# Where the pools of an encoder block's tiles begin in SBUF

## The chip, the core and the metric

The kernel runs on one core of one Trainium2 chip. The metric is the device time of one execution in microseconds (us). A core has five engines that this text names as the profile does: PE (TensorE, the matmuls; PEld is its weight load), DVE (VectorE), ACT (ScalarE), POOL (GpSimd) and SP (SyncE, which here issues DMAs). SBUF is the on-chip memory of 128 partitions; an address in this text is a byte offset within a partition, the same in all 128.

## What is computed

One layer of a bidirectional encoder on 512 positions of width 2048, all in float32, batch 1:

```
h = rmsnorm(x);  z = h @ w_in                       # q latent | kv latent | rope key | conv b, c, h
q, k, v from the latents (8 heads, 128 + 64 rotary dimensions, values 128)
attn = softmax(q k^T / sqrt(192)) v
y = b * conv3(c * h)
x = x + concat(rmsnorm(attn), rmsnorm(y)) @ w_o
u = conv3(rmsnorm(x) @ w_ffn_up) + bias;  g, val = split(u)
x = x + (silu(g) * val) @ w_ffn_down                # d_ff = 5632
out = rmsnorm(x)
```

## The kernel before

The weights lie in DRAM as 375 units of 128 x 1024 float32 (512 KB). A unit is loaded by SP into a tile `raw` (line 261), rounded by ACT to a tile `hi` of the type float32r (line 234), and the remainder `raw - hi` is written by DVE to a tile `lo` (line 231). Activations are split in the same way into pairs of tiles of 128 x 512. A product of two float32 matrices is then three float32r matmuls per block of 128: hi with hi, hi with lo, lo with hi (`mm3`, lines 246 to 250, with the matmul at line 244, and `product`, lines 872 to 881, with the matmul at line 880).

On PE each matmul is two instructions: LDWEIGHTS reads 128 columns (512 bytes of a partition) of the stationary operand, and MATMUL streams the moving operand past it. The moving operand is a whole tile of 512 columns (2048 bytes) in the first part of the program, a half tile of 256 columns (1024 bytes) in the rest. In the profile both operands stand in a matmul's name, `ps<-t,hi`: moving `t`, weights `hi`. `ps<-t` alone means that both operands are `t` tiles.

The program runs through these stages, in this order:

- latent projections, short convolution and attention, output projection, and the first six blocks of the up-projection (line 244, 512 columns wide, but for the values of the attention, lines 547 to 567: there the roles are turned, `hi` and `lo` are the moving operands, 256 columns wide, and the latent's `t` tiles are the weights);
- the other 38 blocks of the up-projection (`up_seven`, line 880): 2 x 2 blocks by seven products in place of eight, moving operands of 256 columns;
- five chunks of the down-projection (`down_seven`, line 880), again by seven products; here each product writes two halves of a PSUM bank, 12 matmuls to each half;
- the last chunk of the down-projection and the final norm (`last_half`, line 244): 256 columns wide, weights and moving operands both in `t` tiles.

The order of the instructions on each engine is fixed by the scheduler when the program is built. What the change touches is where tiles lie. Tile pools take their space in SBUF one behind the other, in the order in which they are opened (lines 174 to 178): `cpool` (constants, vectors of gains), `tp` (80 tiles `t` of 2048 bytes, some of which are named `l`), `sp` (2 small tiles `st`), `wraw` (8 tiles `raw` of 4096 bytes), `wsp` (3 tiles `hi` and 3 tiles `lo` of 4096 bytes). So all `t` tiles have one and the same remainder when their address is divided by 512, and so have all slices of `raw`, `hi` and `lo`, as these are cut at multiples of 512 bytes.

Of the kernel before, what the change touches and what calls it, by code (L numbers as in the profile page):

```python
# [41 lines left out]
F32 = mybir.dt.float32  # L42
# [4 lines left out]
P = 128  # L47
# [15 lines left out]
SCALE = float(1.0 / np.sqrt(np.float32(NOPE + ROPE)))  # L63
UW = 1024
NT = 80
NPLAIN = 6
ORDER = [0, 1, 2, 3, 4]
EARLY = ()
# [103 lines left out]
def encoder_block(ctx: ExitStack, tc: tile.TileContext, gx, wall, vecs, rot, out):  # L172
    nc = tc.nc
    cpool = ctx.enter_context(tc.tile_pool(name="cpool", bufs=1))
    tp = ctx.enter_context(tc.tile_pool(name="tp", bufs=NT))
    sp = ctx.enter_context(tc.tile_pool(name="sp", bufs=2))
    wraw = ctx.enter_context(tc.tile_pool(name="wraw", bufs=8))
    wsp = ctx.enter_context(tc.tile_pool(name="wsp", bufs=3))
    dram = ctx.enter_context(tc.tile_pool(name="dram", bufs=1, space=bass.MemoryType.DRAM))
# [24 lines left out]
    ga = first[:, :KD]  # L204
    vec = cpool.tile([P, NVEC], F32, name="vec")
    nvec = cpool.tile([P, 3 * NF], F32, name="nvec")
    cs = []


# [605 lines left out]
    def up_plain(f, by_half):  # L815

        us, its = [None, None], []
        for s in range(2):
            def conv(ps, s=s):
                t = ztile()  # L820
                us[s] = ztile()
                if s == 0:
                    tt(t, ps, rx.r, ALU.mult)
                else:
                    nc.vector.scalar_tensor_tensor(out=t, in0=ps, scalar=-1.0, in1=rx.r, op0=ALU.mult, op1=ALU.mult)
                conv_up(us[s], t, s, f)

            lag = 5 if (f, s) == (0, 0) else 1
            its.append(proj16([("up", s, f, j) for j in range(2)], h2, [(lag, conv)] + [(lag + 1, lambda ps: gated(us, f))] * s, True))
        return its  # L830
# [121 lines left out]
    def up_seven(f):  # L952
        tg, tv, us = [], [], [None, None]

        def c11(ps):
            tg.append(ztile())
            nc.scalar.copy(out=half(tg[0], 0), in_=ps)

        def c22(ps, other):
            tv.append(ztile())  # L960
            tt(half(tv[0], 1), ps, other, ALU.add)

        def c21(ps, other):
            tt(half(tv[0], 0), ps, other, ALU.add)
            us[1] = ztile()
            conv_up(us[1], tv[0], 1, f)

        def c12(ps):
            nc.scalar.copy(out=half(tg[0], 1), in_=ps)
            us[0] = ztile()  # L970
            conv_up(us[0], tg[0], 0, f)

        units = {f"a{s + 1}{j + 1}": ("up", s, f, j) for s in range(2) for j in range(2)}
        its = seven(f, units, {"c11": c11, "c22": c22, "c21": c21, "c12": c12}, operands)
        its[-1].posts.append((2, lambda: gated(us, f)))
        return its
# [3 lines left out]
    plain = []  # L980
    for f in range(0, NPLAIN - 2):
        plain += [it for its in up_plain(f, False) for it in its]
    four = [it for f in range(NPLAIN - 2, NPLAIN) for it in up_plain(f, True)]
    plain += [its[j] for j in range(2) for its in four]
# [5 lines left out]
    items.extend(plain)  # L990
    for f in range(NPLAIN, NF):
        items.extend(up_seven(f))
# [146 lines left out]
```

## Time and profile before

| | |
|---|---|
| median of 3 runs | 2035.53 us (2034.5 to 2035.62) |
| profiled execution | 2035.79 us, its span 2034.0 us |
| PE busy | 1997.3 us (98%), 13826 matmuls |
| weight loads busy | 1848.2 us (91%) |
| DVE busy | 1542.0 us (76%) |
| ACT busy | 977.4 us (48%) |
| granted PE clock, mean | 0.992 |

The span runs from the first to the last instruction. A share of busy time says how long an engine had something in work; since matmuls are pipelined, the busy time of PE says less than the distance from the start of one matmul to the start of the next, which is had by dividing a stretch by the count of its matmuls. In the rows below "x" stands before a count, times without a unit are us, and PEclk is the granted clock as a share of 2.4 GHz.

### The profile page before, as it was taken

What the parts mean: (1) busy time and instruction counts of PE and PEld (TensorE: products, weight loads), DVE (VectorE), ACT (ScalarE), POOL (GpSimd) and SP (SyncE); (2) the same over time, 40 slices, a digit from 0 to 9 for tenths busy, and PEclk for the clock granted to TensorE, in tenths of its full rate; (3) what the DMA queues carried; (4) which work ended last, traced back from release to release, by engine and by line L of the source; (5) the groups of instructions that cost most, each with busy time, mean ns of one, the idle gap of its engine ahead of it and who ended that gap; (6) DMA issues with size and microseconds to landing.
All of it is one profiled execution on the core that took longest, in us unless ns stands there. A gap on an engine that the chain in (4) does not pass through costs nothing.

```text
span 2034.0 us, 33864 instructions
## 1 busy us (share of the span) xinstructions
PE 1997.3 (98%) x13826; PEld 1848.2 (91%) x13826; DVE 1542.0 (76%) x1893; ACT 977.4 (48%) x1358; POOL 209.6 (10%) x204
## 2 busy tenths in 40 slices
PE   8999999999999999999999999999997999999997
PEld 7888888888888888999999999999997999999997
DVE  7375877664556587788888888888887998987776
ACT  6253534433224344555555555555565554444454
POOL 5001232310001000000000000000010001000000
PEclk9999999999999999999999999999998999999998
DMA  7322222222444344445545545545557776677642
GB/s 259 100 86 78 78 78 73 73 91 95 133 138 140 130 156 138 136 134 152 171 136 151 170 137 150 172 138 148 170 143 219 225 197 172 186 187 199 179 116 83
DMA packets 94155, 290.78 MB, mean 143 GB/s; under 512 B 10672, under 2 KB 18992, under 8 KB 94000
## 3 DMA queue, kind: packets, MB, share of 16 engines
q1 hardware_dynamic: 77648, 230.95, 33.9%
q0 software_dynamic: 16352, 57.68, 13.7%
q8 instruction: 108, 1.77, 0.4%
q14 instruction: 47, 0.39, 0.1%
HBM read 267.62 MB, written 20.97 MB: 142 GB/s over the span
## 4 chain that ended last, share of the span: by engine, by line
PE 90%; DVE 4%; DMA 2%; issue 1%; ACT 0%; SPq 0%; DVEq 0%; ACTq 0%
PE ps L880 50%; PE ps L244 41%; DVE t L231 2%; DMA t<-act 2%; DVE lo L231 2%; DVE raw L231 0%; ACT hi L234 0%; DVE t L846 0%; SPq L787 0%; DVE t L845 0%; SPq L261 0%; DVE t L489 0%; DVEq L1134 0%; ACT ps L931 0%; ACT t L349 0%
## 5 line engine op out<-in xcount | busy, mean ns | idle before, releaser
L880 PE MATMUL ps<-t,hi 128*128 128x256 f32 x6496 | 1118.5, 278 | 17.7 <-ACT hi L234 7.2
L880 PEld LDWEIGHTS ps<-t,hi 128*128 128x128 f32 x6496 | 978.1, 188 | 20.3 <-DVE t L231 8.0
L234 ACT CAST hi<-raw 128x1024 fp32r<-128x1024 f32 (+1 forms) x544 | 568.3, 1047 | 702.9 <-PE ps L244 242.3
L880 PE MATMUL ps<-t,lo 128*128 128x256 f32 x3248 | 884.4, 278 | 1.9 <-DVE lo L231 1.9
L231 DVE TENSOR_TENSOR lo<-raw,hi 128x1024 fp32r<-128x1024 f32 (+1 forms) x543 | 668.4, 1232 | 198.4 <-ACT hi L234 188.3
L244 PE MATMUL ps<-t,hi 128*128 128x512 f32 x2096 | 654.3, 394 | 4.4 <-ACT t L239 3.5
L880 PEld LDWEIGHTS ps<-t,lo 128*128 128x128 f32 x3248 | 602.8, 188 | 2.6 <-DVE lo L231 2.5
L244 PEld LDWEIGHTS ps<-t,hi 128*128 128x128 f32 x2096 | 394.3, 189 | 92.0 <-ACT t L239 4.2
L244 PE MATMUL ps<-t,lo 128*128 128x512 f32 x1056 | 411.4, 392 | 0.0
L231 DVE TENSOR_TENSOR t<-ps,t 128x512 f32<-128x512 f32 (+3 forms) x255 | 143.0, 575 | 152.6 <-PE ps L244 99.8
L231 DVE TENSOR_TENSOR t<-t 128x512 fp32r<-128x512 f32 (+4 forms) x356 | 223.1, 645 | 34.2 <-DMA t<-act 13.2
L244 PEld LDWEIGHTS ps<-t,lo 128*128 128x128 f32 x1056 | 198.9, 188 | 45.0 <-issue 0.5
L231 DVE TENSOR_TENSOR raw<-raw 128x1024 f32<-128x1024 f32 x154 | 187.8, 1219 | 0.5
L244 PE MATMUL ps<-t 128*128 128x256 f32 (+1 forms) x642 | 108.6, 326 | 0.0
L234 ACT CAST t<-t 128x512 fp32r<-128x512 f32 (+2 forms) x149 | 81.3, 577 | 48.8 <-DVE t L231 25.1
L244 PEld LDWEIGHTS ps<-t 128*128 128x128 f32 x642 | 95.1, 190 | 10.3
L231 DVE TENSOR_TENSOR t<-t,ps 128x512 f32<-128x512 f32 x128 | 86.7, 683 | 21.1 <-PE ps L880 19.7
L782 POOL DMA_DIRECT2D act<-t x48 | 27.4, 570 | 694.4 <-DVE t L231 658.9
L231 POOL TENSOR_TENSOR t<-t 128x512 f32<-128x512 f32 x39 | 64.1, 1645 | 72.3 <-DVE t L231 40.5
L904 POOL DMA_DIRECT2D raw<-wall x58 | 50.3, 868 | 163.6 <-ACT t L936 69.4
L910 POOL DMA_DIRECT2D raw<-wall x20 | 17.1, 854 | 316.8 <-DVE lo L231 215.5
L343 ACT ACTIVATE t<-l 128x512 f32<-128x512 f32 x44 | 27.5, 626 | 45.7 <-DVE l L231 45.5
(81 smaller groups left out, 825.3 us busy)
## 6 DMA issues: line engine op xcount, KB each, us to landing
raw<-wall SPq DMA_DIRECT2D x372, 512.0 KB, 4.3
raw<-wall POOLq DMA_DIRECT2D x78, 512.0 KB, 7.4
act<-t POOLq DMA_DIRECT2D x48, 256.0 KB, 2.5
t<-act SPq DMA_DIRECT2D x48, 256.0 KB, 5.1
t<-gx SPq DMA_DIRECT2D x16, 256.0 KB, 3.8
xr<-l POOLq DMA_DIRECT2D x16, 256.0 KB, 2.4
t<-xr SPq DMA_DIRECT2D x16, 256.0 KB, 4.0
t<-xr SPq DMA_DIRECT2D x32, 128.0 KB, 3.9
```

The costliest lines, as they stand in the source:

```text
L231: (eng or nc.vector).tensor_tensor(out=o, in0=a, in1=b, op=op)
L234: nc.scalar.copy(out=dst[0], in_=src)
L244: nc.tensor.matmul(ps, lhsT=w, rhs=x, start=start, stop=stop)
L343: nc.scalar.activation(sq, src, AF.Square)
L782: nc.gpsimd.dma_start(o, t.bitcast(F32))
L880: nc.tensor.matmul(half(ps, e), lhsT=w[a][:, c:c + P], rhs=ops[k][q][b], start=start and e == k == i == 0, stop=k == n - 1 and i == 2, ski ...
L904: nc.gpsimd.dma_start(raw["a21"], wall[UIDX[units["a22"]]], accum_op=ALU.add)
L910: nc.gpsimd.dma_start(raw["s"], wall[UIDX[units["a12"]]], accum_op=ALU.add)
```

## The change

Two things move. `sp` is opened ahead of `tp`, and two tiles that nothing reads or writes take up space: `rest` (912 bytes, the last of `cpool`) and `space` (64 bytes, in a pool `gap` of its own between `tp` and `wraw`).

```diff
+REST = 228
+GAP = 16
...
     cpool = ctx.enter_context(tc.tile_pool(name="cpool", bufs=1))
+    sp = ctx.enter_context(tc.tile_pool(name="sp", bufs=2))
     tp = ctx.enter_context(tc.tile_pool(name="tp", bufs=NT))
-    sp = ctx.enter_context(tc.tile_pool(name="sp", bufs=2))
+    gap = ctx.enter_context(tc.tile_pool(name="gap", bufs=1))
     wraw = ctx.enter_context(tc.tile_pool(name="wraw", bufs=8))
     wsp = ctx.enter_context(tc.tile_pool(name="wsp", bufs=3))
...
     nvec = cpool.tile([P, 3 * NF], F32, name="nvec")
+
+    cpool.tile([P, REST], F32, name="rest")
+    gap.tile([P, GAP], F32, name="space")
     cs = []
```

The addresses in the two built programs:

| tiles | before: first address, remainder by 512 | now: first address, remainder by 512 |
|---|---|---|
| `t`, `l` | 6560, 416 | 7680, 0 |
| `raw` | 170592, 96 | 171584, 64 |
| `hi` | 203360, 96 | 204352, 64 |
| `lo` | 215648, 96 | 216640, 64 |
| `st` | 170400, 416 | 7488, 320 |
| `ones`, `ident`, `first`, `vec`, `nvec` | unchanged | unchanged |

Weights in `hi` or `lo` thus begin 192 bytes behind a moving operand in `t` before (96 - 416 + 512), and 64 bytes behind it now, both by remainders. Two `t` tiles stay 0 apart, and so do two of `raw`, `hi` and `lo`. Divided by 64, all of these addresses have the remainder 32 before and 0 now. No instruction is added or taken away, and none moves: on all five engines the built programs hold the same instructions with the same waits in the same order.

## Rows read from the trace of the kernel before

**Rows 1.** The profile's page: busy time by engine, and the chain by engine.
```profile
PE 1997.3 (98%) x13826; PEld 1848.2 (91%) x13826; DVE 1542.0 (76%) x1893; ACT 977.4 (48%) x1358; POOL 209.6 (10%) x204
...
PE 90%; DVE 4%; DMA 2%; issue 1%; ACT 0%; SPq 0%; DVEq 0%; ACTq 0%
```
**Rows 2.** Chain of waits in order of time: start, length, what, count of instructions.
```profile
46.29 779.53 PE ps L244 x3515
825.81 699.17 PE ps L880 x6169
...
1527.77 5.42 DMA t<-act
...
1572.45 25.72 PE ps L880 x216
...
1685.42 42.44 PE ps L880 x358
...
1766.54 189.74 PE ps L880 x1608
```
**Rows 3.** Windows: PE, PEld, DVE, ACT, POOL busy (count), PEclk, DMA share, GB/s.
```profile
0.00:46.00 46.00, 40.65 (x163) 32.91 (x163) 32.25 (x24) 28.89 (x43) 26.52 (x22) 0.93 0.76 277
550.00:700.00 150.00, 150.00 (x657) 123.06 (x656) 91.91 (x118) 51.93 (x65) 8.98 (x16) 1.00 0.41 139
826.00:1525.00 699.00, 699.00 (x6170) 699.00 (x6169) 578.04 (x625) 403.50 (x552) 54.20 (x76) 1.00 0.53 152
1558.00:1560.00 2.00, 2.00 (x11) 2.00 (x11) 1.97 (x6) 0.62 (x1) 0.00 (x0) 0.50 0.81 274
1766.00:1956.00 190.00, 189.46 (x1607) 189.45 (x1608) 156.39 (x181) 87.00 (x101) 15.82 (x19) 1.00 0.72 194
```
**Rows 4.** Timeline of PE, both operands in t tiles: start, length, what, count.
```profile
197.47 7.41 PE L244 MATMUL ps<-t 128*128 128x512 f32 x32
...
1978.78 21.04 PE L244 MATMUL ps<-t 128*128 128x256 f32 x174
```
**Rows 5.** Timeline of PE, the attention's values (moving hi, weights t), two heads' pairs.
```profile
150.27 0.39 PE L244 MATMUL ps<-hi,t 128*128 128x256 f32 x2
...
151.29 0.39 PE L244 MATMUL ps<-hi,t 128*128 128x256 f32 x2
...
248.98 0.40 PE L244 MATMUL ps<-hi,t 128*128 128x256 f32 x2
...
250.04 0.40 PE L244 MATMUL ps<-hi,t 128*128 128x256 f32 x2
```
**Rows 6.** Timeline of PE in the stretch at half clock.
```profile
1557.46 0.63 PE L880 MATMUL ps<-t,hi 128*128 128x256 f32 x2
...
1559.38 0.63 PE L880 MATMUL ps<-t,hi 128*128 128x256 f32 x2
```
**Rows 7.** Timeline of PEld, weight loads of matmuls one column wide.
```profile
446.29 0.86 PEld L244 LDWEIGHTS ps<-ones,t 128*128 128x128 f32 x7
```
**Rows 8.** Groups by line and shape: busy, mean ns, then idle before and releasers.
```profile
L231 DVE TENSOR_TENSOR lo<-raw,hi 128x1024 fp32r<-128x1024 f32 x537 | 662.5, 1235 | 198.4 <-ACT hi L234 188.3 <-PE ps L244 9.5
L244 PE MATMUL ps<-t,hi 128*128 128x512 f32 x2096 | 654.3, 394 | 4.4 <-ACT t L239 3.5 <-ACT hi L234 0.8
L234 ACT CAST hi<-raw 128x1024 fp32r<-128x1024 f32 x537 | 564.0, 1052 | 691.1 <-PE ps L880 237.1 <-PE ps L244 231.5 <-issue 167.9
L244 PE MATMUL ps<-t,lo 128*128 128x512 f32 x1056 | 411.4, 392 | 0.0
L231 DVE TENSOR_TENSOR raw<-raw 128x1024 f32<-128x1024 f32 x154 | 187.8, 1219 | 0.5
L231 DVE TENSOR_TENSOR t<-t 128x512 f32<-128x512 f32 x111 | 76.5, 698 | 4.4 <-ACT t L343 3.7 <-ACT t L387 0.2
...
L244 PE MATMUL ps<-t 128*128 128x512 f32 x258 | 60.9, 389 | 0.0
...
L244 PE MATMUL ps<-t 128*128 128x256 f32 x384 | 47.8, 284 | 0.0
...
L244 PEld LDWEIGHTS ps<-ones,t 128*128 128x128 f32 x64 | 8.2, 191 | 1.8 <-ACT t L349 0.6 <-POOL t L231 0.5 <-DVE t L231 0.3
```

## The prediction

> **What bounds the kernel now.** I read the page's busy times first: PE is at work for 98% of the span, its weight loads for 91%, DVE for 76%, and the chain that ended last is PE for 90% [rows 1]. Then the chain in order of time: two pieces, 779.53 us of 512-column work and 699.17 us of 256-column work, are PE without a break, and a third of 189.74 us lies in the down-projection [rows 2]. Only between 1525 and 1766 do DVE and transfers stand in the chain between pieces of PE. So the time is the number of matmuls times their spacing, and the views that count are those that give a spacing.
>
> The windows show the clock at full level (1.00, 2.4 GHz) in these stretches [rows 3]. At one column a cycle 256 columns take 106.7 ns and 512 take 213.3 ns. Against that:
>
> - Moving `t`, weights `hi`/`lo` (192 apart), 256 columns: 699.17 us over 6169 matmuls are 113.3 ns in the up-projection; 189.74 over 1608 are 118.0 ns in the down-projection [rows 2].
> - The same pair with 512 columns: 150.00 us with 656 weight loads, 228.7 ns [rows 3].
> - Both in `t` (0 apart): 512 columns, (7.41 - 0.39) / 31 = 226.5 ns, where 0.39 is the length of one such matmul; 256 columns, (21.04 - 0.28) / 173 = 120.0 ns, 0.28 being the length of one [rows 4, 8].
> - Moving `hi`, weights `t` (so 416 - 96 = 320 apart), 256 columns: nine matmuls in 1.02 us, 113.3 ns, at one place, and nine in 1.06 us, 117.8 ns, at another [rows 5].
> - At half clock (0.50, so 1.2 GHz) nine matmuls take 1.92 us, 213.3 ns: exactly the 256 columns, nothing over [rows 3, 6].
>
> Two things follow. What lies above the columns is no fixed cost of an instruction, since it is gone at half clock; it looks like operands that don't come fast enough at full clock. And it depends on where the operands lie: the same 256 columns cost 113.3 or 120.0 ns. In cycles the excess of 113.3, 120.0 and 226.5 is 16, 32 and about 32, and 16 columns of float32 are 64 bytes. So I read it as lumps of 64 bytes, though 118.0 and 228.7 are no whole number of them and must be mixtures (averages of 5/3 and 7/3 lumps).
>
> [...]
>
> **The change part by part.**
>
> *Instructions.* None is added, removed or moved, so there is no wait to follow along a queue; the two new tiles are never written. Cost 0.
>
> *DVE, ACT, POOL.* `raw`, `hi` and `lo` keep their distance to each other (0), `t` tiles to `t` tiles too. DVE takes 1235 ns for 1024 elements from `raw` and `hi`, 1219 ns in place on `raw`, 698 ns for 512 elements of `t` [rows 8]: 521 to 537 ns for the second 512, less than the first 512 cost, so nothing grows with the length as an excess would. I take 0. Even a per cent of them lies beside PE outside the 241 us from 1525 to 1766: at most about 2 us either way.
>
> *Transfers.* In the chain they stand at a few restores of `t` tiles such as 5.42 us [rows 2], 2% of the span [rows 1], about 41 us. A few per cent of that, for rows that begin on a rounder address, would be 1 us. I take 0.
>
> *512-column matmuls.* There are 2096 + 1056 = 3152 with `hi` or `lo` [rows 8]; of the 163 matmuls in the first 46 us, which wait for loads, 16 are the warm-up, so 147 of them don't count [rows 3], and 3005 are left. Bounds: from 228.7 down to the bare 213.3 is 15.4 ns each, 46 us; upward, a lump of 6.7 ns more would be 20 us. Between lies 226.5, the row of the same shape at distance 0, and one lump below that, 219.8, if rows that begin on a multiple of 64 touch one lump fewer. I take the middle of these two, 223.2: 3005 x 5.5 = 17 us saved.
>
> *256-column matmuls in the up-projection.* 6169 at 113.3 ns. Bounds: bare 106.7 saves 41 us, 120.0 costs 41 us. A floor of its own is the weight load: seven loads of one-column matmuls, which stream nothing, follow each other at (0.86 - 0.19) / 6 = 111.7 ns, 0.19 being the mean length of one [rows 7, 8]. So nearly nothing can be had unless the loads too get faster. I take 113.3 as it is, 0 us.
>
> *256-column matmuls in the down-projection.* The pieces of 216, 358 and 1608 run at 119.1, 118.5 and 118.0 ns with their first, longer one [rows 2]: about 2180 matmuls, with smaller pieces between 1565 and 1685 some 2350. The values of the attention show that 113.3 and 118 are two levels of one arrangement, between which chance seems to choose [rows 5]. Bounds: 118.0 to 111.7, 15 us saved, to 120.0, 5 us lost. I take 113.3, the level of the up-projection: 2350 x 4.7 = 11 us saved. DVE is busy 156.39 of 190 us there [rows 3], so it does not take over as the bound.
>
> *Matmuls with both operands in `t`.* Their distance stays 0; only the address modulo 64 changes. There are 384 with 256 columns and 258 with 512 [rows 8]: a lump each would be 4 us. I take 0 and keep them as the test.
>
> Sum: 2035.8 - 17 - 11 = 2008 from the profiled execution's 2035.79, which is 0.3 above the median of the runs; I predict 2009.
>
> **The rivals.**
>
> *A. Some of the excess goes* (as above): 512-column spacing between 219.8 and 226.5, down-projection at 113.3. That is 7 to 27 us and 11 us: 1998 to 2018.
>
> *B. All rows lose a lump.* If the 64-byte remainder is the whole reason, 512 columns come to 222.0 (20 us), up-projection to 111.7 by the floor of the loads (10 us) or to 106.7 if loads lose theirs (41 us), down-projection to the same (15 or 27 us): 45 to 88 us, 1948 to 1991. For it: whole lumps in three of five spacings. Against it: 111.7 ns of the bare loads hold only 5 ns over 106.7, less than a lump, though their weights too begin off a multiple of 64.
>
> [...]
>
> *C. Nothing changes.* If only two classes of distance exist, 0 and other, then 64 behaves as 192 and 320 do. For it: 192 and 320 show the same two levels [rows 2, 5]. Against it: the levels are chosen by something, and any shift can choose anew. 2032 to 2039. [...]
>
> *D. Slower: weights one lump ahead of the moving stream.* Weight load and stream read at the same time. At 192 three lumps lie between them, at 64 only one; if what costs a lump at distance 0 is that both want the same place at the start, 64 is the nearest neighbour of 0 that there is. Then the up-projection goes to 120.0 (+41 us), the down-projection from 118.0 to 120.0 (+5 us), 512 columns to 226.5 (-7 us): 2035.8 + 39 = 2075. A milder form, the up-projection at the 118.0 level, gives +28 us, 2064. It decides from 6169 x 0.67 ns on: when the up-projection's spacing rises by more than 0.7 ns with nothing gained elsewhere. For it: 0 is worse than 192 at 256 columns [rows 2, 4]. Against it: at 512 columns 0 is better than 192 [rows 3, 4].
>
> **How the numbers follow.** A 0.40, B 0.22, C 0.15, D 0.23. The likeliest is A, 2009, its own range 1998 to 2018. The range that holds 8 in 10 leaves out the far half of B (loads speed up too) and of D (120.0 throughout): 1962 to 2066. A measurement of this kernel can tell about 0.2%, 4 us, from no change. Faster takes A and B: 0.62. The same: C, 0.15. Slower: D, 0.23.
>
> **What would show it.** In the profile of the changed kernel: the up-projection's unbroken piece of about 6169 matmuls, divided by its length (113.3 by A and C, 111.7 or less by B, 118 to 120 by D); the down-projection's last piece of about 1608 (113.3 by A, 118.0 by C); a window of 512-column work from 550 to 700 (under 226.5 by A and B, 228.7 by C). The matmuls with both operands in `t` separate the two halves of the change: their distance stays, so if they leave 120.0 and 226.5, the address itself matters; if they stay while the others move, the distance does. DVE's 1235 and ACT's 1052 ns should stay. My forecast is wrong if the up-projection moves at all by more than 1 ns, and its idea is wrong if spacings move by anything that is no part of 6.7 ns.

## The result, and the profile after

The changed kernel takes 2071.39 us (median of 4 runs, 2069.54 to 2072.76) against 2035.57 us of the kernel before: the ratio is 1.0177, its 95% interval 1.0159 to 1.0194. It is slower by 36 us, where 2009 us was forecast, and it lies above the predicted range. The profiled execution took 2072.76 us, its span 2070.9 us, at a mean granted clock of 0.994.

The page's busy times and the chain by engine, as in [rows 1]:

```profile
PE 2034.1 (98%) x13826; PEld 1871.9 (90%) x13826; DVE 1542.9 (75%) x1893; ACT 976.3 (47%) x1358; POOL 209.9 (10%) x204
...
PE 90%; DVE 5%; DMA 2%; issue 1%; ACT 1%; SPq 0%; DVEq 0%; ACTq 0%
```

The instructions are the same in number, and only PE and its weight loads are busy for more than 1 us longer [rows 1]. The chain in order of time (start, length, what, count), as in [rows 2]:

```profile
20.19 819.18 PE ps L250 x3626
839.37 729.17 PE ps L886 x6191
...
1804.51 51.76 PE ps L886 x454
1857.42 135.94 PE ps L886 x1154
```

The 512-column part now ends at 839.37, before at 825.81: +13.6 us. The unbroken piece behind it is the up-projection: 729.17 / 6191 = 117.8 ns a matmul, where 699.17 / 6169 was 113.3 [rows 2]. Over 6169 matmuls the difference is +27.4 us. The last piece of the down-projection has 135.94 / 1154 = 117.8 ns, about as before; the piece ahead of it, 51.76 / 454 = 114.0 ns, does not.

The windows (busy time of PE, PEld, DVE, ACT and POOL with counts, then PEclk, DMA share, GB/s) say the same, at full clock:

```profile
550.00:700.00 150.00, 150.00 (x643) 120.80 (x642) 90.78 (x117) 52.75 (x66) 8.46 (x15) 1.00 0.40 137
560.00:680.00 120.00, 120.00 (x516) 96.86 (x516) 70.08 (x90) 38.99 (x48) 6.29 (x11) 1.00 0.41 140
900.00:1500.00 600.00, 600.00 (x5097) 600.00 (x5096) 480.77 (x518) 332.56 (x456) 43.14 (x61) 1.00 0.49 145
```

The last two windows of the kernel before:

```profile
560.00:680.00 120.00, 120.00 (x526) 98.48 (x525) 73.90 (x95) 41.60 (x52) 7.35 (x13) 1.00 0.41 140
900.00:1500.00 600.00, 600.00 (x5297) 600.00 (x5296) 497.02 (x538) 347.28 (x475) 44.46 (x62) 1.00 0.52 152
```

The first window of the changed kernel holds 642 weight loads for 656 before [rows 3]: 233.6 ns for 228.7. The other two, 120 us of 512 columns and 600 us of the up-projection, are read from the kernels below: the more matmuls a window holds, the shorter their spacing.

What keeps its distance (timeline, with start, length and count; then groups with busy time and mean ns), as in [rows 4, 8]:

```profile
199.98 7.44 PE L250 MATMUL ps<-t 128*128 128x512 f32 x32
...
2016.39 21.04 PE L250 MATMUL ps<-t 128*128 128x256 f32 x174
```
```profile
L237 DVE TENSOR_TENSOR lo<-raw,hi 128x1024 fp32r<-128x1024 f32 x537 | 662.0, 1234 | 222.5 <-ACT hi L240 211.9 <-PE ps L250 9.7
...
L240 ACT CAST hi<-raw 128x1024 fp32r<-128x1024 f32 x537 | 563.3, 1052 | 742.6 <-PE ps L886 262.2 <-PE ps L250 247.0 <-issue 177.6
...
L237 DVE TENSOR_TENSOR raw<-raw 128x1024 f32<-128x1024 f32 x154 | 187.6, 1218 | 0.5
```

Two `t` operands still run at (21.04 - 0.28) / 173 = 120.0 ns and within 1 ns of 226.5; DVE and ACT stand at 1234, 1218 and 1052 ns for 1235, 1219 and 1052. The last stage starts at 2016.39 for 1978.78 [rows 4], +37.6 us. That is +13.6 up to the up-projection, +27.4 in its 6169 matmuls and so -3.4 from there to the last stage; another 0.7 is gained behind, which gives the 36.9 us of the span. The up-projection as a whole takes 740.4 us before (825.81 to 1566.2) and 766.2 after (839.37 to 1605.6), +25.8: 1.6 of the -3.4 us lie in its last 215 matmuls, between waits, and 1.8 in the down-projection. The window of the down-projection, before and then after, shows what became of its spacing there:

```profile
1566.20:1978.70 412.50, 404.67 (x3417) 402.71 (x3416) 357.82 (x461) 200.44 (x254) 34.33 (x41) 1.00 0.68 186
```
```profile
1605.60:2016.30 410.70, 399.26 (x3417) 396.44 (x3416) 357.35 (x461) 200.26 (x254) 34.32 (x41) 1.00 0.69 187
1810.00:1840.00 30.00, 30.00 (x267) 30.00 (x266) 23.98 (x27) 13.62 (x16) 2.58 (x4) 1.00 0.64 173
```

PE is busy for 5.4 us less (its mean spacing, breaks left out, fell from 117.6 to 115.6 ns, with stretches at about 113 like the one from 1810 to 1840), but it stands idle for 11.4 us in place of 7.8, so that only 1.8 us of the gain are left.

### The profile page after: what moved, and what is told of

It is laid out like the page before. It is cut to its first block, busy times and chain, and to the rows that moved or that the text cites. A ratio compares the mean times of both kernels' runs of the same rounds, so it can differ in the third digit from the quotient of the medians.

```text
span 2070.9 us, 33864 instructions
## 1 busy us (share of the span) xinstructions
PE 2034.1 (98%) x13826; PEld 1871.9 (90%) x13826; DVE 1542.9 (75%) x1893; ACT 976.3 (47%) x1358; POOL 209.9 (10%) x204
## 4 chain that ended last, share of the span: by engine, by line
PE 90%; DVE 5%; DMA 2%; issue 1%; ACT 1%; SPq 0%; DVEq 0%; ACTq 0%
PE ps L886 48%; PE ps L250 42%; DVE t L237 2%; DVE lo L237 2%; DMA t<-act 2%; DVE raw L237 1%; DMA l<-gx 0%; ACT hi L240 0%; DMA raw<-wall 0%; DMA t<-xr 0%; DVE t L852 0%; DVE t L851 0%; DVE t L495 0%; SPq L793 0%; DVE t L494 0%
## 5 line engine op out<-in xcount | busy, mean ns | idle before, releaser
L886 PE MATMUL ps<-t,hi 128*128 128x256 f32 x6496 | 1140.1, 281 | 18.2 <-DVE t L237 7.6
L886 PEld LDWEIGHTS ps<-t,hi 128*128 128x128 f32 x6496 | 990.9, 189 | 21.4 <-DVE t L237 8.8
L886 PE MATMUL ps<-t,lo 128*128 128x256 f32 x3248 | 895.0, 281 | 3.1 <-DVE lo L237 3.1
L250 PE MATMUL ps<-t,hi 128*128 128x512 f32 x2096 | 663.6, 399 | 3.4 <-ACT t L245 2.7
L250 PEld LDWEIGHTS ps<-t,hi 128*128 128x128 f32 x2096 | 395.6, 189 | 100.2 <-ACT t L245 3.6
L250 PE MATMUL ps<-t,lo 128*128 128x512 f32 x1056 | 415.6, 396 | 0.0
L237 DVE TENSOR_TENSOR raw<-raw 128x1024 f32<-128x1024 f32 x154 | 187.6, 1218 | 0.5
L788 POOL DMA_DIRECT2D act<-t x48 | 27.4, 570 | 723.6 <-DVE t L237 686.5
```

Of the source, the lines that this page charges most:

```text
L237: (eng or nc.vector).tensor_tensor(out=o, in0=a, in1=b, op=op)
L250: nc.tensor.matmul(ps, lhsT=w, rhs=x, start=start, stop=stop)
L788: nc.gpsimd.dma_start(o, t.bitcast(F32))
L886: nc.tensor.matmul(half(ps, e), lhsT=w[a][:, c:c + P], rhs=ops[k][q][b], start=start and e == k == i == 0, stop=k == n - 1 and i == 2, ski ...
```

## The experiments

All kernels compute the same as the one before; what differs is where tiles lie and, in some, a few extra matmuls whose product is overwritten unread. "Spacing" is the mean from start to start of steady matmuls over a whole stage; 120 and 600 us divided by the counts of the windows come within 1 ns of it, but for the 512 columns of e1 and e9 (below). "Start" is the remainder by 512 of the `t` tiles' address, "distance" by how many bytes `hi` and `lo` begin behind a `t`, by remainders.

| kernel | start, distance | 512 columns, ns | up-projection, ns | us | ratio (95%) |
|---|---|---|---|---|---|
| before | 416, 192 | 229.0 | 113.3 | 2035.5 | |
| after | 0, 64 | 233.3 | 117.8 | 2071.4 | 1.0177 (1.0159-1.0194) |
| e1 | 0, 192 | 229.7 | 117.8 | 2063.2 | 1.0138 (1.0123-1.0153) |
| e2 | 416, 64 | 233.3 | 113.3 | 2045.2 | 1.0048 (1.0033-1.0063) |
| e3 | 0, 0 | 226.9 | 120.0 | 2076.2 | 1.0203 (1.0186-1.0220) |
| e4 | 0, 256 | 226.9 | 120.0 | 2076.1 | 1.0199 (1.0182-1.0216) |
| e5 | 0, 64, entry moved | 233.3 | 117.8 | 2070.6 | 1.0173 (1.0157-1.0188) |
| e6 | 0, 64, 38 extra | 233.3 | 113.4 | 2051.5 | 1.0075 (1.0060-1.0090) |
| e7 | 416, 128 | 232.4 | 118.7 | 2081.5 | 1.0223 (1.0206-1.0240) |
| e8 | 416, 224 | 233.3 | 116.7 | 2069.9 | 1.0164 (1.0149-1.0179) |
| e9 | 0, 192, 3 extra | 229.7 | 117.8 | 2065.2 | 1.0147 (1.0131-1.0163) |
| e10 | before, 16 extra | 229.0 | 113.3 | 2035.6 | 1.0000 (0.9991-1.0009) |
| e11 | 480, 0 then 192, extra | 226.8 | 117.8 | 2058.9 | 1.0120 (1.0106-1.0134) |
| e12 | 480, 0 then 64, 4 extra | 226.8 | 113.4 | 2028.3 | 0.9968 (0.9959-0.9978) |
| e13 | 96, 192 | 229.0 | 117.8 | 2062.3 | 1.0133 (1.0119-1.0147) |
| e14 | 256, 192 | 229.0 | 117.8 | 2062.3 | 1.0136 (1.0121-1.0152) |
| e15 | 416, 192, entry moved | 229.0 | 117.8 | 2062.1 | 1.0133 (1.0119-1.0146) |

**One half of the change at a time.** In e1 the tiles begin at multiples of 512 and the distance stays 192; in e2 the start is the old one and the distance is the new one.

```diff
-GAP = 16          # e1, against after
+GAP = 48
-REST = 228        # e2, against after
+REST = 80
```

> The change with 192 bytes in place of 64 between the end of the t tiles and the weights' pools (GAP = 48): t tiles at multiples of 512, weights 192 behind. Theory 1, the distance modulo 512 between weights and moving tiles sets the spacing and the address itself does not: as before, 2036 us, 256 columns in the up-projection at 113.3 ns, 512 columns at 228.7 ns. Theory 2, the rounder start address is what costs: as with the change, 2071 us, 117.8 and 233.3 ns. Theory 3, any new layout draws the levels anew by chance: anything between 2030 and 2075, with the up-projection at either 113.3 or 117.8.

> The other half alone: t tiles at the remainder 416 by 512 as before (REST = 80), weights 64 behind them as with the change. Theory 1 (distance): 2071 us, 117.8 ns in the up-projection and 233.3 ns for 512 columns. Theory 2 (address): 2036 us, 113.3 and 228.7 ns. Theory 3 (chance): anything between.

The windows of e1, then of e2:

```profile
560.00:680.00 120.00, 120.00 (x526) 98.44 (x526) 72.57 (x94) 41.06 (x51) 6.88 (x13) 1.00 0.41 140
900.00:1500.00 600.00, 600.00 (x5097) 600.00 (x5096) 478.08 (x515) 331.62 (x455) 43.02 (x60) 1.00 0.51 148
```
```profile
560.00:680.00 120.00, 120.00 (x516) 96.70 (x515) 70.26 (x90) 38.97 (x48) 6.28 (x11) 1.00 0.42 139
900.00:1500.00 600.00, 600.00 (x5296) 600.00 (x5295) 496.02 (x536) 345.80 (x474) 45.90 (x64) 1.00 0.53 152
```

In this window the 512-column spacing follows the distance (526 matmuls at 192, 516 at 64, whatever the start). Over the whole stage e1 is 0.7 ns slower than the kernel before, because it holds a second level here too. The kernel before, and then e1, further ahead and at the entry into the up-projection:

```profile
460.00:530.00 70.00, 70.00 (x308) 57.43 (x306) 32.38 (x38) 19.03 (x23) 0.00 (x0) 1.00 0.32 106
```
```profile
822.22 0.62 PE L244 MATMUL ps<-t,hi 128*128 128x512 f32 x2
...
825.65 0.39 PE L880 MATMUL ps<-t,hi 128*128 128x256 f32 x2
```
```profile
460.00:530.00 70.00, 70.00 (x301) 56.70 (x301) 33.34 (x41) 19.99 (x23) 0.00 (x0) 1.00 0.31 102
```
```profile
825.10 0.63 PE L250 MATMUL ps<-t,hi 128*128 128x512 f32 x2
...
828.60 0.40 PE L886 MATMUL ps<-t,hi 128*128 128x256 f32 x2
```

The last 15 matmuls of 512 columns take 3.43 us in the kernel before, 228.7 ns each, and 3.50 us in e1, 233.3 ns each, at the same distance. So 233.3 ns, the spacing at 64, also occurs at 192, in pieces; at 64 no stretch of the four kernels (after, e2, e5, e6) was faster than that. The up-projection seemed to follow the start: 5097 matmuls at 0, 5296 at 416. That reading was tested by two more starts at distance 192.

```diff
-    cpool.tile([P, REST], F32, name="rest")   # e13: start 96, with GAP = 48
-REST = 228                                    # e14: start 256, with GAP = 48
+REST = 164
```

> All tiles moved together: t at the remainder 96 by 512, weights 192 behind as before. If the remainder by 64 of the start chooses the level (32 here as before): 113.3 ns, 2036 us. If only the state at the entry does, either level: 2036 or 2063 us. 512 columns at 228.9 to 229.7 ns in any case.

> All tiles moved together: t at the remainder 256 by 512, weights 192 behind as before. If the remainder by 64 of the start chooses the level (0 here, as in e1): 117.8 ns, 2063 us. If only the state at the entry does: 2036 or 2063 us. A pair 2036 (e13) and 2063 (this) speaks for the remainder, any other pair against it.

Windows of e13, then of e14:

```profile
550.00:700.00 150.00, 150.00 (x657) 123.09 (x656) 90.11 (x116) 51.52 (x64) 9.02 (x16) 1.00 0.43 141
900.00:1500.00 600.00, 600.00 (x5097) 600.00 (x5096) 480.06 (x517) 333.03 (x456) 43.13 (x60) 1.00 0.50 147
```
```profile
550.00:700.00 150.00, 150.00 (x657) 123.10 (x656) 91.15 (x117) 51.52 (x64) 9.00 (x16) 1.00 0.41 139
900.00:1500.00 600.00, 600.00 (x5097) 600.00 (x5096) 479.86 (x517) 332.30 (x455) 43.02 (x60) 1.00 0.50 148
```

Both stay at 117.8 ns and 2062.3 us. Divided by 64 these starts have the remainders 32 and 0, so rounder addresses give nothing. Three of four starts had the slow spacing, which left two theories: 416 is special, or something else than addresses decides.

**The distance alone.** e3 leaves the second tile out, e4 makes it 256 bytes; e7 and e8 keep the old start.

```diff
-    gap.tile([P, GAP], F32, name="space")     # e3
-GAP = 16                                      # e4: 64; with REST = 80 e7: 32, e8: 56
+GAP = 64
```

> The change without the 64-byte tile: weights 0 apart from the moving tiles. Theory 1 with the rows of before in which both operands are t tiles: 256 columns at 120.0 ns, 512 columns at 226.6 ns everywhere; against the profile of the change that is +2.2 ns x about 8500 = +19 us and -6.8 ns x 3005 = -20 us, so about 2070 us. If what the t tiles show is peculiar to them (they are not rewritten between matmuls): something else, 113 to 118 ns. Theory 3 (chance): the up-projection at 113.3 or 117.8 again.

> Weights 256 bytes behind the moving tiles (GAP = 64). Theory 1 has no row for it. If the wheel that matters is 512 bytes long and 0 is the worst place at 256 columns, half a turn away is the best: up-projection at 113.3 ns or less, 512 columns at 228.7 or less, 2036 us or less. If the wheel is 256 bytes long: as at distance 0, 120.0 and 226.6 ns, about 2070 us. Theory 2 (address alone): 2071 us.

> t tiles at the remainder 416 as before (REST = 80), weights 128 behind (GAP = 32). Distances 0 and 256 gave the same 120.0 and 226.7 ns, so the wheel is taken to be 256 bytes long, and 128 is as far from 0 as one can be. If the cost falls with the distance from 0: 256 columns at 113.3 ns or below throughout, 512 columns at 228.9 ns or below, 2025 us or less. If the wheel is 128 bytes long after all: 120.0 and 226.7 ns, 2075 us. If the two levels are there at every distance but 0: 113.3 or 117.8 in the up-projection, 2030 to 2070 us.

> t tiles at the remainder 416, weights 224 behind (GAP = 56), which on a wheel of 256 bytes is 32 ahead of 0, and no multiple of 64. 512 columns went from 233.3 ns at 64 over 228.9 at 192 to 226.7 at 256; if that goes on evenly, 224 gives about 227.8 ns, and 256 columns lie between 113.3 and 120.0. If only multiples of 64 matter (the low bits are dropped), 224 behaves as 192: 228.9 ns, and 113.3 or 117.8. Total 2030 to 2070 us, by the level of the up-projection.

Windows of e3, e4, and the up-projection's of e7 and e8:

```profile
560.00:680.00 120.00, 120.00 (x531) 99.38 (x530) 74.60 (x96) 42.59 (x54) 7.91 (x14) 1.00 0.44 144
900.00:1500.00 600.00, 600.00 (x5002) 600.00 (x5001) 470.54 (x507) 323.66 (x447) 43.02 (x60) 1.00 0.49 144
```
```profile
560.00:680.00 120.00, 120.00 (x531) 99.38 (x530) 74.31 (x97) 42.50 (x53) 7.91 (x14) 1.00 0.42 141
900.00:1500.00 600.00, 600.00 (x5002) 600.00 (x5002) 471.57 (x507) 323.56 (x447) 43.03 (x60) 1.00 0.49 143
```
```profile
900.00:1500.00 600.00, 600.00 (x5058) 600.00 (x5058) 476.37 (x514) 329.48 (x453) 43.12 (x60) 1.00 0.50 145
```
```profile
900.00:1500.00 600.00, 600.00 (x5145) 600.00 (x5144) 485.01 (x522) 337.13 (x461) 44.56 (x62) 1.00 0.51 147
```

e3 turns the weights into what two `t` tiles are, 0 apart, and gets their figures, 120.0 and 226.9 ns (two `t` tiles of the kernel before: 120.0 and 226.5 [rows 4]): at this distance the kind of tile made no difference. 256 gives the same as 0, in both spacings and in the whole. 128 and 224 give further spacings of 256 columns, 118.7 and 116.7 ns, neither 113.3 nor 120.0. No case of e7's expectation had 118.7 or the 2081.5 us; 116.7 lies in the range that one case of e8's gave, but its 512 columns came to 233.3 ns, not 227.8.

**What chooses between 113.3 and 117.8.** e5 and e15 leave every address alone and move the two matmuls of `mark` (512 columns, both operands in `t`), which stand 24 matmuls ahead of the second part of the up-projection, to its very start: e5 in the kernel after, e15 in the one before. On PE nothing else moves. e6 adds one extra matmul of that kind for each of the 38 blocks. In the list of items it stands ahead of its block; in the trace the first one stands at the entry, the second 48 matmuls behind it and each further one 168 behind the last, so inside the block before. e9 to e12 have theirs at such places too.

```diff
-    plain[-2].posts.append((0, mark))         # e5 and e15
+    plain[-1].posts.append((0, mark))
+        items.append(Item(lambda _, b=f % 2: mm(banks[b], h2[0][0][:, :P], h2[0][0], True, True)))   # e6, ahead of up_seven(f)
```

> The changed kernel with every address as it is; the two 512-column matmuls that fill two PSUM banks for the seven products (mark) are issued behind the last item of the plain up-projection, not ahead of it, so PE comes into the 256-column work from two matmuls with both operands in t tiles. The output is the same. Theory A, at distances 64 and 192 the 256-column spacing has two levels, 113.3 and 117.8 ns, and PE keeps for 700 us the one into which it falls at the entry: the level can come out as 113.3, then 2071 - 27 = 2044 us, or again as 117.8, 2071 us; nothing between, and no other spacing. Theory B, a start at a multiple of 64 itself gives 117.8 ns: 2071 us, 117.8 ns whatever the entry. The 512-column spacing stays 233.3 ns in both.

> The changed kernel with one more 512-column matmul of two t tiles ahead of each of the 38 blocks of seven products (into the PSUM bank that is overwritten next; the output is the same): 38 new entries in place of one, at a price of 38 x 0.23 = 9 us. Theory A (level kept from the entry): some of the 38 blocks of 19 us come out at 113.3 ns, some may stay at 117.8, each block at one level; between 2053 us (all low) and 2080 us (all high). Theory B (the address itself): all blocks at 117.8 ns, 2080 us.

> The kernel before, every address as it is, with the edit of e5: the two 512-column matmuls of t tiles stand directly ahead of the up-projection's 256-column work. If the addresses choose the level: 113.3 ns, 2036 us. If the state at the entry does, it can be 117.8 ns: 2063 us; then the time before was itself one of two. If it stays at 113.3, that does not exclude the entry.

The timeline of e6 around its second extra matmul:

```profile
842.06 0.40 PE L886 MATMUL ps<-t,hi 128*128 128x256 f32 x2
...
843.12 0.39 PE L250 MATMUL ps<-t 128*128 128x512 f32 x1
843.35 0.39 PE L886 MATMUL ps<-t,hi 128*128 128x256 f32 x2
...
844.37 0.39 PE L886 MATMUL ps<-t,hi 128*128 128x256 f32 x2
```

Nine matmuls from 842.06 to 843.12 take 1.06 us, 117.8 ns each; nine from 843.35 to 844.37 take 1.02, 113.3 ns, and all later blocks keep that. One matmul in between has switched the level for 650 us. The price of the extra ones, 38 x 0.23 us, is 9 us; the gain is more.

e5 switched nothing: its piece stays at 729.17 / 6191 = 117.8 ns.

```profile
839.35 729.17 PE ps L886 x6191
```

e15 did; its chain and its window:

```profile
46.05 779.52 PE ps L244 x3515
825.57 678.42 PE ps L880 x5760
```
```profile
900.00:1500.00 600.00, 600.00 (x5097) 600.00 (x5096) 479.54 (x516) 332.14 (x456) 43.03 (x60) 1.00 0.51 148
```

The addresses of the kernel before, and its 512-column stage to within 0.3 us [rows 2], but then 678.42 / 5760 = 117.8 ns, and 2062.1 us in the whole: what e1, e13 and e14 gave at their starts. So 416 is not special, and the level isn't chosen by addresses alone. The kernel before happens to enter the up-projection so that it gets the cheaper one.

The traces show one sign of it ahead of the entry. In e1, e9, e13 and e14 the 24 matmuls between `mark` and the entry run at 233.3 ns, though those ahead of `mark` run at 229, and 117.8 ns follows; in the kernel before and e10 they stay at 229.2 ns, and 113.3 follows. In e15 they run at 229.2 as well, but then `mark` itself comes, and 117.8 follows. All seven are at distance 192. This is an agreement over seven kernels; no run shows it to be the cause.

Can the extra matmul be used at distance 192? e9 is e1 with one ahead of the first three blocks; e10 is the kernel before with one ahead of each of the 16 groups of four chunks of the down-projection (four a chunk).

```diff
+        if f < NPLAIN + 3:                    # e9, ahead of up_seven(f)
+            items.append(Item(lambda _, b=f % 2: mm(banks[b], h2[0][0][:, :P], h2[0][0], True, True)))
+                items.append(Item(lambda _, b=m % 2: mm(banks[b], h2[0][0][:, :P], h2[0][0], True, True)))   # e10
```

> The layout of e1 (t tiles at multiples of 512, weights 192 behind; 2063 us, up-projection at 117.8 ns) with one more 512-column matmul of two t tiles ahead of the first three of the 38 blocks; the output is the same. Theory A (two levels at one layout, the state at the entry decides): one of the three knocks PE to 113.3 ns, where it stays: 2063 - 27 = 2036 us, as before. If the start at a multiple of 512 holds the level: 2064 us, 117.8 ns throughout.

> The kernel before, its addresses as they are, with such a matmul ahead of each group of four products' halves in the first four chunks of the down-projection (16 of them, 4 us), where it runs at 117.8 ns. Theory A: part of the down-projection's 3360 matmuls falls to 113.3 ns; at most 2500 x 4.4 - 4 = 7 us saved (2029 us), at worst nothing falls and the 4 us are lost (2040 us). If the level belongs to the stage and not to the entry: 117.8 ns stays, 2040 us.

No: e9 keeps 703.74 / 5975 = 117.8 ns behind its third extra matmul.

```profile
854.32 703.74 PE ps L886 x5975
```

In e10 the chain's piece in the down-projection is

```profile
1857.03 96.34 PE ps L880 x818
```

which is 117.8 ns still. At this distance the extra matmul switched nothing, in either place. The 16 of e10 cost nothing that the runs can tell (2035.6 us), where 4 us were expected.

**Two distances in one kernel.** The table suggests 0 apart for 512 columns and 113.3 ns for the rest. Weights go into wider tiles, and the up- and down-projections use them further in; `sp` becomes a part of the tile `nvec` to make room.

```diff
-        hi = wsp.tile([P, UW], F32R, tag="hi", name="hi")
+        hi = wsp.tile([P, UW + 64], F32R, tag="hi", name="hi")[:, :UW]            # 512 columns; lo alike
-            hi = wsp.tile([P, UW], F32R, tag="hi", name="hi")
+            hi = wsp.tile([P, UW + 64], F32R, tag="hi", name="hi")[:, 48:48 + UW]  # e11; e12: [:, 16:16 + UW]
```

e11 (192 apart in the second part) has the extra matmuls of e9 and e10, e12 (64 apart) one ahead of each of the first four blocks of the up-projection.

> hi and lo get 256 bytes more each; while matmuls are 512 columns wide the weights lie 0 behind the moving tiles (by remainders of 256), in the seven products 192 behind, and the extra matmuls of e9 and e10 are in. The small tiles st of the norms share one tile with nvec, to make room. Expected from the rows of e3 and e1: 512 columns at 226.9 in place of 228.9 ns, 3000 x 2.1 = 6 us saved; up-projection at 113.3 ns; down-projection as in e10; values 192 x 5 ns = 1 us lost. 2023 to 2035 us, faster than before by 0 to 12 us. If distance is not what sets the 512-column spacing: 228.9 or 233.3 ns there and no gain.

> e11 with 64 in place of 192 bytes between weights and moving tiles in the seven products, extra matmuls ahead of the first four blocks of the up-projection (as in e6, where the second one brought 113.3 ns at distance 64), none in the down-projection. 512 columns at 226.9 ns (6 us saved against before), up-projection at 113.3 ns (as before), down-projection at 114.7 ns in the mean as in e2 and e6 (2400 x 2.9 = 7 us saved), 1 us lost at the values, 1 us for the extra matmuls: 2024 us. If the extra matmuls don't bring 113.3 this time: 2052 us.

Windows of e11, and the chain and windows of e12:

```profile
560.00:680.00 120.00, 120.00 (x531) 99.38 (x530) 74.62 (x96) 42.54 (x53) 7.93 (x14) 1.00 0.43 143
900.00:1500.00 600.00, 600.00 (x5097) 600.00 (x5096) 480.89 (x518) 333.19 (x457) 43.12 (x60) 1.00 0.50 145
```
```profile
821.26 5.66 PE ps L879 x48
...
1968.70 40.91 PE ps L244 x340
```
```profile
560.00:680.00 120.00, 120.00 (x531) 99.38 (x530) 74.33 (x97) 42.49 (x53) 7.93 (x14) 1.00 0.43 140
900.00:1500.00 600.00, 600.00 (x5297) 600.00 (x5295) 497.13 (x538) 346.84 (x475) 46.53 (x65) 1.00 0.52 151
```

Both get the 226.8 ns in the first part. e11 fell to 117.8 in the second, as every kernel at 192 but the one before and e10. e12 begins at 117.8 (48 matmuls in 5.66 us), is switched by its second extra matmul as e6 was, and keeps 113.4. It takes 2028.33 us (11 runs, 2024.20 to 2033.42): 0.3% less than the kernel before, and the only version whose interval lies below it; 2024 had been expected. In the profiled execution, which at 2025.13 us is one of the faster ones, the up-projection begins 4.5 us sooner than before (821.26 for 825.81) and the last stage 10 us sooner (1968.70 for 1978.78); about 6 us of that are the down-projection at a mean of 114.7 ns for 117.6.

## Why the prediction was wrong

*The idea of rounder addresses.* The step that failed is "if rows that begin on a multiple of 64 touch one lump fewer", which carried the -17 us of the 512-column matmuls. The `t` pairs, kept as the test, moved by less than 1 ns, and e13 and e14 (remainders 32 and 0 by 64) agree to 0.1 ns. The spacing went with the distance: 229.0 ns at 192 became 233.3 at 64, at both starts (after, e2), which is +14 us. My bound of +20 us held this; the value was on the wrong side of 0. The sign that I had set for the idea, moves that are no part of 6.7 ns, tells little: both levels lie 4.4 ns apart, two thirds of it, and no run shows that anything comes in lumps of 64 bytes: that was an estimate of mine from five spacings. The bare 106.7 ns under it is what the rows give: 213.3 ns for 256 columns at the granted clock 0.50 [rows 3, 6], and at full clock, 0 apart, 226.5 - 120.0 = 106.5 ns for 256 columns more [rows 4].

*The up-projection.* "I take 113.3 as it is, 0 us" measured +27.4. I had seen two levels in [rows 5] and the lower one throughout the up-projection [rows 2], and took that for a property of the layout. e15 shows that it belongs to the program's entry into that stage: moving two matmuls ahead of it, at unchanged addresses, costs the same 27 us. Rival D's milder form had this size (+28 us), but its time of 2064 left out the loss at 512 columns, and it was right by luck and not for its reason: it took 64 for a near neighbour of 0, and e2 and e6 run at 113.3 and 113.4 ns with weights 64 apart.

*The down-projection.* -11 us became -1.8, with 1.6 more saved at the end of the up-projection. Part of it ran at the 113.3 that I took for all of it, and the last piece stayed at 117.8; of the 5.4 us that PE was busy for less, 3.6 went into longer idle times between its pieces. I had priced the spacing alone there, though the chain of that stretch holds DVE and transfers too.

*What held.* The zeros for DVE, ACT, transfers and `t` pairs. Rival C said against itself that "any shift can choose anew": that was the larger half of the loss, and I gave it no price. Rival B is refuted: in no kernel did 256 columns come to 111.7 or 106.7 ns in the up-projection.

The two halves of the loss come apart by the kernels at equal level. At 113.3 ns, 192 apart takes 2035.5 us and 64 apart 2045.2 (e2); at 117.8 ns, 2062.1 to 2063.2 (e1, e13 to e15) and 2070.6 to 2071.4 (e5, after). So the distance of 64 costs 7 to 10 us in the whole (its loss at 512 columns less what the down-projection gains), and the level 25 to 28 us.

e2 and e3 differ in layout alone, and 233.3 became 226.9 ns and 113.3 became 120.0: the spacing is not free of where weights and moving operand lie.

*Open.* What in the entry chooses the level, why the start of the tiles changes what `mark` does to it, and why an extra matmul switches it at 64 but not at 192, was not found. Whether 512 columns have a cheaper level at 64, as they have at 192, no run shows; if they have, the +14 us are a level too. By what means the distance acts on the spacing, no row shows.

## What to carry to other kernels

Where PE is the bound, read the spacing of matmuls from start to start, stage by stage, and treat the distance between weights and moving operand as a parameter to be tried, apart for each width of the moving operand. Before a gain or loss is put down to a layout, disturb the entry of the stage (move a matmul, add one) at the same addresses: a long unbroken stretch can hold either of two levels (here 113.3 ns for 699 us or 117.8 for 729), and one timing of one program can't tell these from the layout. A level seen in one profile is not a term that may be taken as fixed.

## What the hardware showed unexpectedly

- The spacing of float32r matmuls at full clock (1.00) differed in these kernels with how far weights and moving operand lie apart, and was alike at 0 and 256 bytes: 512 columns take 226.9 ns at 0 and 256, 229.0 or, in pieces, 233.3 at 192, 232.4 at 128, 233.3 at 64 and 224; 256 columns take 120.0 at 0 and 256, 118.7 at 128, 116.7 at 224, and 113.3 or 117.8 at 64 and 192.
- Of the distances tried, what is best for one width is worst for the other: 0 and 256 give the lowest spacing at 512 columns (226.9 ns) and the highest at 256 (120.0 ns).
- PE kept one of two levels, 113.3 or 117.8 ns, for 600 us and more without a break, and all runs of one program agreed to 0.5%, so the level went with the program and not with the run. One extra matmul switched it from 117.8 to 113.4 ns at distance 64 (e6, e12), each time the second one.
